# A hybrid decoder block: each head's values projected ahead of its keys, scores kept times -1/8, and the softmax factor taken from two scalars

## The chip, the core and the metric

The kernel is written in a tile language for one NeuronCore of a Trainium2 chip and runs on one of its cores. The metric is the device time of one execution in microseconds (us). The engines named here are TensorE (PE, its weight loads PEld), VectorE (DVE), ScalarE (ACT), GpSimd (POOL) and SyncE (SP, which issues most transfers). Each runs its own queue in order and waits for the others by semaphores.

## The reference, cut to what matters

One layer on 1,024 tokens behind 16 meta tokens (1,040 columns), width 1,024: an RG-LRU branch, a differential attention branch, a gated merge, a squared-ReLU MLP. The change lies in the attention: 8 heads, two key and query parts of 64 columns each (c = 0, 1), 128 value columns, blocks of 128 queries.

```
q = _rope(q, cos, sin);  k = _rope(k, cos, sin)
s = jnp.einsum('bqhcd,bkhcd->bhcqk', q, k) * scale          # scale = 1/8
s = jnp.where(mask, s, finfo.min)
p = jax.nn.softmax(s, axis=-1)
p_diff = p[:, :, 0] - lam * p[:, :, 1]
o = jnp.einsum('bhqk,bkhe->bqhe', p_diff, v)
```

## The kernel before, in words

Every fp32 matmul is made of three, of high and low fp32r parts. A loaded weight tile w_raw is split by POOL: w_hi (L106), then w_lo (L115), two passes over 128x1024. The loads follow a list, `todo`, one tile ahead, so a projection's first matmul sets off the split for the next projection but one tile.

In the attention stage PE's order is the program's own (pinned). For each head, `head_inputs(h)` is a generator of 88 steps, each step three matmuls: 32 for the keys (four chunks of 260 columns), 32 for the values, 24 for the queries (chunks of 504, 260, 260). Keys and queries end in `rope`: ACT copies the last chunk to `raw`, SP swaps halves into `sw` by four transfers, DVE multiplies `raw` by cos (L470), POOL multiplies `sw` by sin (L471) and, for keys, adds the two (L472); then ACT casts the high parts of the keys (L480) and POOL subtracts twice for the low parts (L481, 64x1040 each). The values are copied to `vt` and must be transposed in blocks by PE; an ACT cast and a DVE subtraction (L515, L516) move each group of three out of PSUM. The transposes use the one of two projection banks that the running chunk does not use, and the next chunk needs that bank again.

While head h is attended to, the inputs of head h+1 are woven in as filling: the lists `MAIN`, `MAIN_FIRST`, `MAIN_LAST` and `TAIL` give how many of the steps stand behind each step of the attention. Eighteen (34 at the start) are done before a head's main part begins.

The attention of head h goes by query blocks b = 0 to 7. `scores` makes, for each part c and each piece of up to 512 keys, a matmul pair into one of three score banks; DVE moves the piece out with the mask added and its row maximum kept (L548). A small reduction (L553) and a small multiplication by -1/8 (L554) give the bias, ACT takes the exponentials with row sums (L556), DVE forms a factor from the sums (reciprocal L561, L562) and blends the two parts (L564, both operands in SBUF); the meta columns are cast and subtracted apart (L570, L571, 32 columns). `turn` transposes blended blocks, ACT casts them (L588), DVE subtracts (L589), and `weigh` multiplies them with the values. PE's score of piece n waits until DVE has emptied the score bank of piece n-3.

DVE, ACT, POOL and SP queues are ordered by a scheduler from a model of times; they are in order once built.

Of the kernel before, what the change touches and what calls it, by code (L numbers as in the profile page):

```python
# [13 lines left out]
AF = mybir.ActivationFunctionType  # L14
ALU = mybir.AluOpType
# [3 lines left out]
P = 128  # L19
D = 1024  # L20
# [16 lines left out]
ALL = [(0, 260), (260, 260), (520, 260), (780, 260)]  # L37
REAL = [(NM, 504), (520, 260), (780, 260)]
CH2 = [(0, 512), (512, 512)]
MASK = -3.0e38  # L40
# [30 lines left out]
def hybrid_block(ctx: ExitStack, tc: tile.TileContext, x, meta_tokens, g_mix, w_in, conv_w, conv_b,  # L71
# [3 lines left out]
    V, A, G, PE = nc.vector, nc.scalar, nc.gpsimd, nc.tensor  # L75
# [8 lines left out]
    def f32(ap):  # L84
        return ap.bitcast(F32)
# [15 lines left out]
    def fix(i):  # L101
        if fixed[0]:
# [4 lines left out]
                                                op1=ALU.add)]  # L107
# [11 lines left out]
    todo = []  # L119
# [3 lines left out]
    for d in range(KT):  # L123
        todo += [(w_rnn_out, P * d)] + [(w_in, 5 * D + P * (d + 3))] * (d + 3 < KT)
    for h in range(NH):
        todo += [(w_in, c * D + P * h) for c in (3, 4, 2)]
    todo += [(w_in, 6 * D + P * d) for d in range(KT)]
    todo += [(w_attn_out, P * d) for d in range(KT)]
    todo += [(w_o, j) for j in range(KT // 2)]
# [59 lines left out]
    lam2 = const.tile([P, 2], F32, name="lam2")  # L189
# [20 lines left out]
    sums = [const.tile([P, NH, NB], F32, name=f"sum{c}") for c in range(2)]  # L210
# [4 lines left out]
    with tc.tile_pool(name="hn", bufs=1, reuse_waits="tile") as hnp:  # L215
# [6 lines left out]
        with tc.tile_pool(name="pre", bufs=2) as pre:  # L222
# [19 lines left out]
            for i, (rows, col, src) in enumerate(blocks):  # L242
# [11 lines left out]
                else:  # L254
                    V.scalar_tensor_tensor(out=xg[:rows], in0=xt[:rows], scalar=r[:rows], in1=gbc[:rows],
                                           op0=ALU.mult, op1=ALU.mult)
# [167 lines left out]
        with tc.tile_pool(name="atc", bufs=1, reuse_waits="tile") as atc, \  # L424
# [52 lines left out]
            def set_keys(h, t1):  # L477
                k2 = keys[h] = [at.tile([P, T], F32R, name=f"k2{c}", bufs=2) for c in range(2)]
                for c, (own, oth) in enumerate(halfs):
                    A.copy(out=k2[c][own], in_=t1[own])  # L480
                    G.tensor_tensor(out=k2[c][oth], in0=t1[own], in1=f32(k2[c][own]), op=ALU.subtract)  # L481

            def head_inputs(h):


                yield from rope(h, 3 * D + P * h, ALL, lambda t1: set_keys(h, t1))

                vt = at.tile([P, T], F32, name="raw", bufs=2)
                vm = at.tile([P, 2, 2, NM], F32R, name="vm")

                def use(t0, w, o):
                    A.copy(out=vt[:, t0:t0 + w], in_=o)
                    if t0 == 0:
                        meta = o[:, None, :NM].to_broadcast((P, 2, NM))
                        A.copy(out=vm[:, :, 0, :], in_=meta)
                        V.tensor_tensor(out=vm[:, :, 1, :], in0=meta, in1=f32(vm[:, :, 0, :]), op=ALU.subtract)

                yield from project_by(4 * D + P * h, ALL, take_g, use)
                vv = vals[h] = at.tile([P, NB, 2, P], F32R, name="v", bufs=2)
                for step, _ in enumerate(rope(h, 2 * D + P * h, REAL, lambda t1: rot.update({h: t1}), V)):  # L500
                    yield
                    if step % 8 != 3:
                        continue
                    js = range(step // 8 * 3, step // 8 * 3 + 3)
                    o = take_g(1).rearrange("p (a e) -> p a e", e=P)
                    for i, j in enumerate(js):
                        if j < NB:
                            transpose(o[:, i, :], vt[:, NM + P * j:NM + P * (j + 1)])
                        else:
                            transpose(o[:4 * NM, i, :], f32(vm).rearrange("p a b c -> p (a b c)"))  # L510
                            vt_meta[h] = vmts[h % 2]
                            A.copy(out=vt_meta[h][:4 * NM], in_=o[:4 * NM, i, :])
                    n = min(3, NB - js[0])
                    dst = vv[:, js[0]:js[0] + n]
                    A.copy(out=dst[:, :, 0, :], in_=o[:, :n, :])  # L515
                    V.tensor_tensor(out=dst[:, :, 1, :], in0=o[:, :n, :], in1=f32(dst[:, :, 0, :]), op=ALU.subtract)  # L516

            def queries(h):

# [6 lines left out]
                    V.tensor_tensor(out=qls[c][own], in0=t1[own], in1=f32(q2[c][own]), op=ALU.subtract)  # L526

            def scores(h, b, st):

                L = NM + P * (b + 1)  # L530
                np_ = -(-L // 512)
                cuts = [L * i // np_ // 2 * 2 for i in range(np_ + 1)]
                mx = small.tile([P, 2, 3], F32, name="mx")
                m2 = small.tile([P, 2], F32, name="m2")
                sc = []
                for c in range(2):
                    s = at.tile([P, T], F32, name=f"s{c}", bufs=3 - c)
                    sc.append(s)
                    for i in range(np_):
                        k0, w = cuts[i], cuts[i + 1] - cuts[i]  # L540
                        wa = max(w, 256)
                        o = take_s()
                        matmul(o[:, :wa], lhsT=qls[c][:, P * b:P * (b + 1)], rhs=keys[h][c][:, k0:k0 + wa],
                               start=True, stop=False)
                        matmul(o[:, :wa], lhsT=ques[h][c][:, P * b:P * (b + 1)], rhs=keys[h][c][:, k0:k0 + wa],
                               start=False, stop=True)
                        m0 = MZ + P - w if i == np_ - 1 else 0
                        V.tensor_tensor_reduce(  # L548
                            out=s[:, k0:k0 + w], in0=o[:, :w], in1=mask[:, m0:m0 + w],
                            op0=ALU.add, op1=ALU.max, scale=1.0, scalar=MASK, accum_out=mx[:, c, i:i + 1])  # L550
                        if c == 0 or i < np_ - 1:
                            yield
                V.tensor_reduce(out=m2, in_=mx[:, :, :np_], op=ALU.max, axis=mybir.AxisListType.X)  # L553
                V.tensor_scalar(out=m2, in0=m2, scalar1=-0.125, scalar2=None, op0=ALU.mult)  # L554
                for c in range(2):
                    A.activation(out=sc[c][:, :L], in_=sc[c][:, :L], func=AF.Exp, scale=0.125, bias=m2[:, c:c + 1],  # L556
                                 accum_out=sums[c][:, h, b:b + 1])

                s0, s1 = sc
                cf = small.tile([P, 1], F32, name="cf")  # L560
                V.reciprocal(out=cf, in_=sums[1][:, h, b:b + 1])  # L561
                V.scalar_tensor_tensor(out=cf, in0=sums[0][:, h, b:b + 1], scalar=lam2[:, 0:1], in1=cf,  # L562
                                       op0=ALU.mult, op1=ALU.mult)
                V.scalar_tensor_tensor(out=s0[:, :L], in0=s1[:, :L], scalar=cf, in1=s0[:, :L],  # L564
                                       op0=ALU.mult, op1=ALU.add)
                st[b] = s0

                st["dm", b] = dm = at.tile([P, 2, 2, NM], F32R, name="dm", bufs=3)
                meta = s0[:, None, :NM].to_broadcast((P, 2, NM))
                V.tensor_copy(dm[:, 0], meta)  # L570
                V.tensor_tensor(out=dm[:, 1], in0=meta, in1=f32(dm[:, 0]), op=ALU.subtract)  # L571
                yield
# [492 lines left out]
    with tc.tile_pool(name="mlp", bufs=1, reuse_waits="tile") as ml:  # L1065
# [24 lines left out]
        for c in range(last + 1):  # L1090
            b = {}
# [105 lines left out]
```

## Time and profile before

| what | value |
|---|---|
| three runs, median (lowest, highest) | 1895.49 us (1891.83, 1895.86) |
| the profiled execution: time, span | 1891.57 us, 1889.8 us |
| PE busy over the span | 1786.3 us, 95% |
| DVE, ACT, POOL busy | 1200.3, 800.6, 660.4 us |
| instructions | 25963 |
| mean granted TensorE clock | 0.984 of full speed |

PE is the engine that is nearly always busy, so time is saved or lost where it stands idle or runs at the lower clock. Busy shares of the other engines are averages over stages; whether one of them holds PE up is read from PE's gaps and from what ends them.

### The profile page before, as it was taken

Reading aid. Unit: us, or ns where it says so; the run is one execution under the profiler, and the core shown is the slowest. Engines: PE = TensorE matmul, PEld = TensorE weight load, DVE = VectorE, ACT = ScalarE, POOL = GpSimd, SP = SyncE. Lnnn points to the kernel's source line nnn. Section 1 sums busy time; section 2 is a strip of 40 time slices with the busy share of each in tenths; the row PEclk is TensorE's granted clock in tenths of the full one; section 3 lists DMA queues with packets and bytes.
Section 4 is the critical chain, followed back from the end, with each engine's and each line's share of the span. In section 5 each row is a group of like instructions: output and inputs, shape, how many; then the busy total and the mean of one; then the engine's idle time right before and its main releaser. Section 6 shows DMA issues by size and latency. Waiting matters only on the chain.

```text
span 1889.8 us, 25963 instructions
## 1 busy us (share of the span) xinstructions
PE 1786.3 (95%) x10178; PEld 1565.2 (83%) x10178; DVE 1200.3 (64%) x1829; ACT 800.6 (42%) x1421; POOL 660.4 (35%) x433
## 2 busy tenths in 40 slices
PE   5999999999889989999999999988999988999998
PEld 5999988889789888988889888867888877888876
DVE  7688882112877788788753544475443435888887
ACT  5566660002455545555543210465454453333343
POOL 3243320016332443334312331047656554313220
PEclk9999999999999999999999999999999999999999
DMA  4111112232121122112216535324455568543423
GB/s 158 44 35 46 45 34 73 73 101 82 40 54 43 46 57 60 43 40 54 65 54 253 179 118 191 119 86 161 160 182 172 184 209 301 192 140 133 159 102 119
DMA packets 182236, 208.16 MB, mean 110 GB/s; under 512 B 8048, under 2 KB 137296, under 8 KB 178656
## 3 DMA queue, kind: packets, MB, share of 16 engines
q1 hardware_dynamic: 163376, 171.35, 28.0%
q10 hardware_dynamic: 18736, 35.13, 5.0%
q8 instruction: 80, 1.31, 0.3%
q14 instruction: 44, 0.36, 0.1%
HBM read 147.60 MB, written 50.40 MB: 105 GB/s over the span
## 4 chain that ended last, share of the span: by engine, by line
PE 68%; DVE 19%; issue 6%; ACT 3%; DMA 2%; POOL 1%; SPq 0%; DVEq 0%; POOLq 0%; ACTq 0%
PE bank L155 66%; DVE s L548 2%; PE bank L160 2%; DVE s L564 2%; DVE cf L562 2%; DVE t L470 1%; DVE sl L1100 1%; ACT s L556 1%; DVE ql L526 1%; DMA w_raw<-in_w_in 1%; DVE gate L381 1%; DVE w_lo L115 1%; ACT th L1099 1%; DVE gate L380 0%; DVE m L554 0%
## 5 line engine op out<-in xcount | busy, mean ns | idle before, releaser
L106 POOL TENSOR_SCALAR w_hi<-w_raw 128x1024 fp32r<-128x1024 f32 x77 | 92.0, 1194 | 597.6 <-PE bank L155 471.2
L155 PE MATMUL bank<-act0l,w_hi 128*128 128x260 f32 (+2 forms) x768 | 268.2, 349 | 2.7 <-DVE c L885 2.0
L155 PE MATMUL bank<-act0h,w_lo 128*128 128x260 f32 (+2 forms) x768 | 263.4, 343 | 4.8 <-DVE w_lo L115 4.8
L155 PE MATMUL bank<-act0h,w_hi 128*128 128x260 f32 (+2 forms) x768 | 262.5, 342 | 0.0
L155 PE MATMUL bank<-act1l,w_hi 128*128 128x260 f32 x896 | 255.6, 285 | 0.6 <-POOL w_hi L106 0.6
L155 PE MATMUL bank<-act1h,w_lo 128*128 128x260 f32 x896 | 254.0, 283 | 0.0
L155 PE MATMUL bank<-act1h,w_hi 128*128 128x260 f32 x896 | 253.3, 283 | 0.0
L155 PE MATMUL bank<-th,sl 128*128 128x512 f32 x432 | 169.9, 393 | 1.7 <-DVE sl L1100 1.4
L155 PEld LDWEIGHTS bank<-act1l,w_hi 128*128 128x128 f32 x896 | 169.8, 189 | 2.0 <-POOL w_hi L106 0.9
L155 PEld LDWEIGHTS bank<-act1h,w_lo 128*128 128x128 f32 x896 | 169.6, 189 | 1.2 <-DVE w_lo L115 0.2
L155 PEld LDWEIGHTS bank<-act1h,w_hi 128*128 128x128 f32 x896 | 169.6, 189 | 0.0
L155 PE MATMUL bank<-th,sh 128*128 128x512 f32 x432 | 169.1, 391 | 0.0
L155 PE MATMUL bank<-tl,sh 128*128 128x512 f32 x432 | 162.3, 393 | 4.7 <-DVE tl L1100 4.7
L155 PEld LDWEIGHTS bank<-act0h,w_lo 128*128 128x128 f32 x768 | 147.9, 193 | 19.2 <-DVE w_lo L115 5.6
L155 PEld LDWEIGHTS bank<-act0l,w_hi 128*128 128x128 f32 x768 | 147.8, 192 | 17.9 <-DVE c L885 2.5
L155 PEld LDWEIGHTS bank<-act0h,w_hi 128*128 128x128 f32 x768 | 148.0, 193 | 16.3
L115 DVE TENSOR_TENSOR w_lo<-w_raw,w_hi 128x1024 fp32r<-128x1024 f32 x60 | 83.8, 1396 | 81.3 <-POOL w_hi L106 76.7
L556 ACT ACTIVATE s<-s,m 128x272 f32<-128x272 f32 (+7 forms) x128 | 99.9, 783 | 71.4 <-DVE m L554 71.1
L548 DVE CUSTOM_DVE_ANT_0 s<-bank,mask 128x144 f32<-128x144 f32 (+6 forms) x224 | 109.1, 504 | 31.2 <-PE bank L155 29.7
L155 PE MATMUL bank<-k,ql 128*128 128x256 f32 (+6 forms) x224 | 76.5, 345 | 29.1 <-DVE mx L548 28.4
L1100 DVE TENSOR_TENSOR sl<-s_raw,sh 128x2048 fp32r<-128x2048 f32 x27 | 101.4, 3755 | 0.0
L155 PEld LDWEIGHTS bank<-tl,sh 128*128 128x128 f32 x432 | 81.7, 189 | 22.8 <-DVE tl L1100 5.6
(336 smaller groups left out, 4368.8 us busy)
## 6 DMA issues: line engine op xcount, KB each, us to landing
w_raw<-in_w_in SPq DMA_DIRECT2D x56, 512.0 KB
s_raw<-ff_d SPq DMA_DIRECT2D x27, 1024.0 KB
ff_d<-r ACTq DMA_DIRECT2D x16, 1024.0 KB
b<-in_w_ff SPq DMA_DIRECT2D x16, 1024.0 KB
w_raw<-in_w_ff SPq DMA_DIRECT2D x16, 512.0 KB
s_raw<-in_w_ff SPq DMA_DIRECT2D x16, 512.0 KB
ff_d<-r ACTq DMA_DIRECT2D x31, 256.0 KB
s_raw<-in_w_ff SPq DMA_DIRECT2D x17, 256.0 KB
```

The lines of the kernel that those rows point to most:

```text
L106: hi_part = [lambda out, in_: G.tensor_scalar(out=out, in0=in_, scalar1=1.0, scalar2=0.0, op0=ALU.mult, op1=ALU.add)]
L115: fix(low_part[0].tensor_tensor(out=lo, in0=raw, in1=f32(hi), op=ALU.subtract))
L155: i = PE.matmul(*args, skip_group_check=skip[0], **kw)
L160: i = PE.transpose(o, x, ident[:x.shape[0], :x.shape[0]])
L381: V.tensor_tensor_scan(out=rt, data0=s2, data1=it, initial=0.0, op0=ALU.mult, op1=ALU.add)
L470: V.tensor_tensor(out=t1[:, ts], in0=raw[:, ts], in1=cos[:, ts], op=ALU.mult)
L526: V.tensor_tensor(out=qls[c][own], in0=t1[own], in1=f32(q2[c][own]), op=ALU.subtract)
L548: V.tensor_tensor_reduce(out=s[:, k0:k0 + w], in0=o[:, :w], in1=mask[:, m0:m0 + w], op0=ALU.add, op1=ALU.max, scale=1.0, scalar=MASK, accu ...
L556: A.activation(out=sc[c][:, :L], in_=sc[c][:, :L], func=AF.Exp, scale=0.125, bias=m2[:, c:c + 1], accum_out=sums[c][:, h, b:b + 1])
L562: V.scalar_tensor_tensor(out=cf, in0=sums[0][:, h, b:b + 1], scalar=lam2[:, 0:1], in1=cf, op0=ALU.mult, op1=ALU.mult)
L564: V.scalar_tensor_tensor(out=s0[:, :L], in0=s1[:, :L], scalar=cf, in1=s0[:, :L], op0=ALU.mult, op1=ALU.add)
L1100: ordered(V.tensor_tensor(out=hl[1], in0=src, in1=f32(hl[0]), op=ALU.subtract))
```

## The change

Three edits. In `head_inputs` the values are projected first, and their transposes stand among the keys' 32 steps (behind the fifth, thirteenth and twenty-first) rather than among the queries' 24; the list of loads follows. L548's operation adds the mask, multiplies by -1/8 and keeps the minimum, so the bias needs no multiplication (64 small DVE instructions go), and where one piece covers a block's keys (blocks 0 to 2) no reduction (24 go). L562's product is made by a tensor_scalar with two scalar operands instead of an operation with two tensor operands.

```diff
     for h in range(NH):
-        todo += [(w_in, c * D + P * h) for c in (3, 4, 2)]
+        todo += [(w_in, c * D + P * h) for c in (4, 3, 2)]
...
             def head_inputs(h):
-                yield from rope(h, 3 * D + P * h, ALL, lambda t1: set_keys(h, t1))
-
                 vt = at.tile([P, T], F32, name="raw", bufs=2)
...
                 yield from project_by(4 * D + P * h, ALL, take_g, use)
                 vv = vals[h] = at.tile([P, NB, 2, P], F32R, name="v", bufs=2)
-                for step, _ in enumerate(rope(h, 2 * D + P * h, REAL, lambda t1: rot.update({h: t1}), V)):
+
+                for step, _ in enumerate(rope(h, 3 * D + P * h, ALL, lambda t1: set_keys(h, t1))):
                     yield
-                    if step % 8 != 3:
+                    if step % 8 != 3 or step // 8 == 3:
                         continue
...
                     V.tensor_tensor(out=dst[:, :, 1, :], in0=o[:, :n, :], in1=f32(dst[:, :, 0, :]), op=ALU.subtract)
+                yield from rope(h, 2 * D + P * h, REAL, lambda t1: rot.update({h: t1}), V)
...
-                            op0=ALU.add, op1=ALU.max, scale=1.0, scalar=MASK, accum_out=mx[:, c, i:i + 1])
+                            op0=ALU.add, op1=ALU.min, scale=-0.125, scalar=-MASK, accum_out=mx[:, c, i:i + 1])
...
-                V.tensor_reduce(out=m2, in_=mx[:, :, :np_], op=ALU.max, axis=mybir.AxisListType.X)
-                V.tensor_scalar(out=m2, in0=m2, scalar1=-0.125, scalar2=None, op0=ALU.mult)
+                if np_ > 1:
+                    V.tensor_reduce(out=m2, in_=mx[:, :, :np_], op=ALU.min, axis=mybir.AxisListType.X)
                 for c in range(2):
-                    A.activation(out=sc[c][:, :L], in_=sc[c][:, :L], func=AF.Exp, scale=0.125, bias=m2[:, c:c + 1],
+                    low = m2[:, c:c + 1] if np_ > 1 else mx[:, c, 0:1]
+                    A.activation(out=sc[c][:, :L], in_=sc[c][:, :L], func=AF.Exp, scale=-1.0, bias=low,
                                  accum_out=sums[c][:, h, b:b + 1])
...
-                V.scalar_tensor_tensor(out=cf, in0=sums[0][:, h, b:b + 1], scalar=lam2[:, 0:1], in1=cf,
-                                       op0=ALU.mult, op1=ALU.mult)
+                V.tensor_scalar(out=cf, in0=sums[0][:, h, b:b + 1], scalar1=lam2[:, 0:1], scalar2=cf,
+                                op0=ALU.mult, op1=ALU.mult)
```

What this does to the queues is seen in three places of one head. The first is DVE's queue in the third block of the attention (128x264 are pieces of block 3, s_6708 with 400 columns is block 2). Before:

```order
L470 TENSOR_TENSOR t_6492<-raw,cos 128x1040
L548 ISA s_6786,mx<-bank_6787,mask 128x264
L548 ISA mx 128x1
L548 ISA s_6786,mx<-bank_6791,mask 128x264
L548 ISA mx 128x1
L561 RECIPROCAL cf<-sum_116 128x1
L553 TENSOR_REDUCE m_6747<-mx 128x2
L562 SCALAR_TENSOR_TENSOR cf<-sum_115,lam_81,cf 128x1
L554 TENSOR_SCALAR m_6747<-m_6747 128x2
L564 SCALAR_TENSOR_TENSOR s_6708<-s_6716,cf,s_6708 128x400
```

DVE's queue at the same place with the change (its line numbers differ by one or two: L549 is L548, L566 is L564; s_6672 is block 2, s_6710 block 3, s_6817 the first piece of block 4):

```order
L564 TENSOR_SCALAR cf<-sum_115,lam_81,cf 128x1
L555 TENSOR_REDUCE m_6709<-mx 128x2
L566 SCALAR_TENSOR_TENSOR s_6672<-s_6680,cf,s_6672 128x400
L572 CAST dm<-s_6672 128x32
L573 TENSOR_TENSOR dm<-s_6672,dm 128x32
L563 RECIPROCAL cf<-sum_116 128x1
L564 TENSOR_SCALAR cf<-sum_115,lam_81,cf 128x1
L515 TENSOR_TENSOR v<-bank_6765,v 128x3x128
L566 SCALAR_TENSOR_TENSOR s_6710<-s_6737,cf,s_6710 128x528
L572 CAST dm<-s_6710 128x32
L573 TENSOR_TENSOR dm<-s_6710,dm 128x32
L549 ISA s_6817,mx<-bank_6818,mask 128x328
```

The keys' cosine product has left the place, and the values' first subtraction (L515) now stands there, behind block 3's factor. The second place is DVE's queue where block 5 is blended and block 6 begins (128x784 and 128x456). Before:

```order
L561 RECIPROCAL cf<-sum_116 128x1
L562 SCALAR_TENSOR_TENSOR cf<-sum_115,lam_81,cf 128x1
L548 ISA s_7043,mx<-bank_7044,mask 128x456
L548 ISA mx 128x1
L564 SCALAR_TENSOR_TENSOR s_6956<-s_6968,cf,s_6956 128x784
L548 ISA s_7043,mx<-bank_7065,mask 128x456
```

The same place on DVE with the change:

```order
L564 TENSOR_SCALAR cf<-sum_115,lam_81,cf 128x1
L470 TENSOR_TENSOR t_6724<-raw,cos 128x1040
L566 SCALAR_TENSOR_TENSOR s_6922<-s_6934,cf,s_6922 128x784
L549 ISA s_7021,mx<-bank_7022,mask 128x456
L549 ISA mx 128x1
L549 ISA s_7021,mx<-bank_7042,mask 128x456
L549 ISA mx 128x1
L572 CAST dm<-s_6922 128x32
L549 ISA s_7046,mx<-bank_7047,mask 128x456
L549 ISA mx 128x1
L573 TENSOR_TENSOR dm<-s_6922,dm 128x32
L549 ISA s_7046,mx<-bank_7051,mask 128x456
```

Both the keys' cosine product and block 5's blend now stand ahead of the first move of block 6's scores. The third place is POOL's queue with the change, from the split that the queries' first step sets off (w_hi) on:

```order
L106 TENSOR_SCALAR w_hi<-w_raw 128x1024
L115 TENSOR_TENSOR w_lo<-w_raw,w_hi 128x1024
L471 TENSOR_TENSOR sw<-sw,sin 128x1040
L589 MEMSET pth 128x128
L472 TENSOR_TENSOR t_6724<-t_6724,sw 128x1040
L589 MEMSET ptl 128x128
L481 TENSOR_TENSOR k_6993<-t_6724,k_6993 64x1040
```

Before, the keys' four passes (L471, L472, L481 twice) stood behind the split that the values' first step set off; now they stand behind that of the queries' first step, 32 steps later.

## Rows read from the trace of the kernel before

**Rows 1.** The page's first section: busy us, share of the span, instructions.

```profile
PE 1786.3 (95%) x10178; PEld 1565.2 (83%) x10178; DVE 1200.3 (64%) x1829; ACT 800.6 (42%) x1421; POOL 660.4 (35%) x433
```

**Rows 2.** PE in order of time: start, length, [idle before, releaser].

```profile
483.52 0.90 PE L160 MATMUL bank<-ident,s 128*128 128x128 f32 x3 [3.94 <-DVE s L564]
...
560.24 0.42 PE L155 MATMUL bank<-k,ql 128*128 128x328 f32 x1 [3.69 <-DVE mx L548]
...
683.38 0.40 PE L155 MATMUL bank<-pth,v 128*128 128x256 f32 x2
...
690.94 0.58 PE L155 MATMUL bank<-k,ql 128*128 128x328 f32 x1 [3.65 <-DVE mx L548]
...
702.42 0.28 PE L155 MATMUL bank<-act1h,w_hi 128*128 128x260 f32 x1
...
707.01 0.47 PE L155 MATMUL bank<-k,ql 128*128 128x456 f32 x1 [0.63 <-DVE mx L548]
...
711.47 0.40 PE L155 MATMUL bank<-pth,v 128*128 128x256 f32 x2
...
716.42 0.32 PE L155 MATMUL bank<-k,ql 128*128 128x346 f32 x1
```

**Rows 3.** DVE and POOL in order of time, at the gap before 690.94.

```profile
680.81 2.40 POOL L115 TENSOR_TENSOR w_lo<-w_raw,w_hi 128x1024 fp32r<-128x1024 f32 x1
...
681.00 3.30 DVE L470 TENSOR_TENSOR t<-raw,cos 128x1040 f32<-128x1040 f32 x1
...
684.36 2.43 POOL L471 TENSOR_TENSOR sw<-sw,sin 128x1040 f32<-128x1040 f32 x1 [1.16 <-DVE t L470]
...
685.12 1.69 DVE L562 SCALAR_TENSOR_TENSOR cf<-sum,lam,cf 128x1 f32<-128x1 f32 x1
...
686.85 2.85 DVE L564 SCALAR_TENSOR_TENSOR s<-s,cf,s 128x400 f32<-128x400 f32 x1
686.88 2.39 POOL L472 TENSOR_TENSOR t<-t,sw 128x1040 f32<-128x1040 f32 x1
...
690.38 0.49 DVE L548 CUSTOM_DVE_ANT_0 s<-bank,mask 128x328 f32<-128x328 f32 x1
```

**Rows 4.** Two stretches behind that gap: us, PE, PEld, DVE, ACT, POOL, clock, DMA share, GB/s.

```profile
692.00:694.00 2.00, 2.00 (x12) 2.00 (x11) 2.00 (x10) 0.59 (x1) 0.00 (x0) 0.50 0.00 0
694.00:696.00 2.00, 2.00 (x17) 2.00 (x17) 0.64 (x3) 1.84 (x4) 0.00 (x0) 0.89 0.00 0
```

**Rows 5.** DVE and POOL at the end of the queries' projection, in order of time.

```profile
724.40 1.05 POOL L106 TENSOR_SCALAR w_hi<-w_raw 128x1024 fp32r<-128x1024 f32 x1 [17.73 <-PE bank L155]
724.75 1.77 DVE L470 TENSOR_TENSOR t<-raw,cos 128x1024 f32<-128x1024 f32 x1 [0.52 <-ACT raw L465]
725.54 3.22 POOL L115 TENSOR_TENSOR w_lo<-w_raw,w_hi 128x1024 fp32r<-128x1024 f32 x1
...
727.05 1.99 DVE L622 TENSOR_TENSOR sql<-sq,sqh 128x256 fp32r<-128x256 f32 x1
```

**Rows 6.** Two small DVE operations, all heads: count, shortest/median/longest in ns.

```profile
L562 DVE SCALAR_TENSOR_TENSOR cf<-sum,lam,cf x64: 212/220/2347, 479.6 to 978.3; 128x1 f32<-128x1 f32 x64
...
L570 DVE CAST dm<-s x64: 168/181/2317, 482.4 to 980.1; 128x32 fp32r<-128x32 f32 x64
```

**Rows 7.** Groups by form in one head, 672 to 737: count, busy us, mean ns.

```profile
L562 DVE SCALAR_TENSOR_TENSOR cf<-sum,lam,cf 128x1 f32<-128x1 f32 x8 | 5.9, 737 | 0.2
L589 DVE TENSOR_TENSOR ptl<-bank,pth 128x512 fp32r<-128x512 f32 x6 | 3.9, 680 | 0.0
...
L548 DVE CUSTOM_DVE_ANT_0 s<-bank,mask 128x456 f32<-128x456 f32 x4 | 2.4, 620 | 0.0
...
L554 DVE TENSOR_SCALAR m<-m 128x2 f32<-128x2 f32 x8 | 1.8, 227 | 0.1
...
L564 DVE SCALAR_TENSOR_TENSOR s<-s,cf,s 128x784 f32<-128x784 f32 x1 | 1.0, 1024 | 0.0
...
L556 ACT ACTIVATE s<-s,m 128x912 f32<-128x912 f32 x2 | 2.1, 1050 | 0.5 <-DVE m L554 0.5
```

## The prediction

> **What bounds the kernel now.** I read the busy times first: PE works for 95% of the span, every other engine for less than two thirds [rows 1]. So I looked next, in PE's order of time over the attention stage, for the places where PE stands idle. The reader is to see there a gap of 3.94 us in the first head and then, once a head, one of 3.65 to 3.8 us, of which the first and the fourth head's stand here, always before a score of block 4 that waits for DVE to empty a score bank [rows 2]. A smaller one of 0.63 us stands in block 6. Then I read what DVE and POOL did before the long gap. DVE's cosine product of the keys (L470) is called at 681.00 and takes 3.30 us, while POOL's w_lo runs until 683.21: the product itself is some 1.1 us, the rest is waiting for POOL. The tiny L562 ends with POOL's L471 at 686.8, the blend L564 runs only when L472 is over at 689.27, and the move that PE waits for comes behind it, at 690.38 [rows 3]. A DVE operation with two operands in SBUF and a POOL pass take turns here, whole operation by whole operation. Last the clock: PE runs at half (1.2 of 2.4 GHz) for the two microseconds from 692, and is back during the next two [rows 4]; counted from 690.94 that is about 3.4 us at half, 1.7 us lost. The keys' place therefore costs a head 3.65 + 1.7 = 5.35 us.
>
> **What the change takes away there.** Steps 1 to 14 of a head's main part are now values, so L470, L471, L472 and both L481 leave blocks 3 and 4. POOL keeps w_hi and w_lo there. What is new is the values' first group: its transposes come behind the fifth keys' step, and the ninth step needs that bank back. PE had done eight filling steps when its weigh began at 683.38 [rows 2]; the last of these eight is now that ninth keys' step, so PE asks for the bank at about 683.4. DVE's subtraction for it (L515) is behind block 2's blend, which waits for w_lo until 683.21 [rows 3], behind two small operations, and behind the factor of block 3, whose exponentials I put at an end of about 683.6 (an estimate). That puts its end at about 685.1: a gap of 1.75 us is my value. It is 0 if the blend gets in before w_lo, and as much as the old 3.65 at the other end. I count no loss of clock for it: the rows show half clock only behind 3.65 us. Saved: 5.35 - 1.75 = 3.6 us a head.
>
> **The small operations.** Eight L554 a head (227 ns each) go, and L562 (737 ns in the mean over eight, where its median over all heads is 220) loses an operand [rows 6, 7]. They stand ahead of exponentials and blends on DVE, under PE's work; off the path they are worth nothing. Behind the first place they bring blocks 4 and 5 forward; I give 0.5 us a head, between 0 and the 1.8 us that L554 sums to.
>
> **What the change puts into block 6.** The keys now end just before block 6, where the values ended. Set 0 at the end of that last matmul (702.70 before). PE had used up its three score banks at 706.38, 3.7 us later, and in the old order had to wait only 0.63 us [rows 2]. In the new order of DVE, L470 and block 5's blend stand ahead of the first move of block 6.
>
> L470 meets the w_hi that the same matmul sets off. The queries' end shows this very pairing: L470 waits for w_hi's end, runs, w_lo waits for L470 and then takes 2.2 us of its own, and a later two-operand subtraction waits for w_lo [rows 5]. So w_hi ends at 1.2, L470 at 2.3, w_lo at 4.5, the blend of 784 columns (1.02) at 5.5, the first move (0.62) at 6.1 [rows 7]. PE's fourth score waits 2.4 us.
>
> POOL's L471 follows from 5.5 to 7.9 (2.43) [rows 3], L472 from 8.1 to 10.5. Between the moves stand a 32-column cast and a 32-column subtraction. Such a cast takes 0.18 us alone but up to 2.3 us behind POOL [rows 6]; here the cast is held to 7.9 and the subtraction to 10.5. So the fourth move ends at 11.3 and the subtraction L589 for the transposed blocks (0.68 [rows 7], behind another that I put at 0.4) at 12.5. PE needs 4.46 us from its fourth score to that weigh, of which 0.3 were transposes now done earlier [rows 2]: it is there at 10.2 and waits 2.3 us.
>
> The exponentials of block 6 (two of 1.05) run from 11.5 to 13.7, behind them a cast on ACT and the next L589, to 14.9; PE is there at 13.5 and waits 1.4 us. Then the blend to 16.0, and POOL's two key passes (2.43 each, rows 7) to 18.4 and 21.0; the next cast waits for the first, the next subtraction for the second, with block 7's first moves behind each. The second ends at 21.7. From that weigh to block 7's fifth score PE has 4.95 us of its own [rows 2], 18.9 with the gap so far: 2.8 us more.
>
> Together 2.4 + 2.3 + 1.4 + 2.8 = 8.9 us of gaps where there were 0.63: 8.3 more. Against 3.6 and 0.5 a head is 4.2 us longer. No half clock is counted behind these gaps; if gaps of 2.4 us bring it too, up to 1.7 us a head more shows, since most of it would lie under the next wait. If the small subtractions slip through between two passes, about 3 us a head less. SP's transfers move with the keys: four swaps behind the same copy, landing before POOL is free of w_lo, so they cost nothing; were they 1 us later, L471 would start that much later. The keys themselves are due only a head's tail later: cover of some 15 us.
>
> **The sum.** Six heads weave the next head's inputs by the same list: 6 x 4.2 = 25 us. The first head has its own list, with the keys at blocks 0 to 2 before and at block 5 now: it loses 3.94 us and a half clock of about 1.7, and takes on up to 8.3; I put 0, between -5.6 and +8.3. The last head weaves no keys: 0, at best -1.8. The profiled execution took 1891.6 us, span 1889.8: 1891.6 + 25 = 1917 us. It stands 3.9 us under the median of the runs, at their lower end; I leave the sum as it is.
>
> **Rivals.** *The waits go with the operand (faster).* Place: the factor before each blend. If what holds L562 up is its second operand, and the blends find POOL between passes, eight factors give DVE back 8 x (0.737 - 0.220) = 4.1 us a head [rows 6, 7], the moves behind them come in time at block 6 too, and both of PE's gaps go: 6 x (5.35 + 0.63) = 36 us, 1856 us; with a part of it, 1870 to 1885. It decides whether block 6's first move ends by 3.7 us after the keys' last matmul. Against it: the blend at 686.85 waited 2.4 us right behind an L562 that had waited too [rows 3], and L470 now stands in front. The Trainium skill (SBUF — State Buffer, "Who interferes with whom") says that a DVE instruction with two SBUF inputs contends with a GpSimd instruction that reads SBUF, and one with at most one SBUF input outside the two-port modes does not; the trace agrees for L470 and the blend, and no row here shows the new form of the factor. By that rule the factor stops waiting, which is what this rival builds on. Chance 0.2.
>
> *The blend gets in before w_lo (slower, but little).* If DVE keeps its turn behind L470, block 5's blend ends at 3.4, the first move at 4.0 and the fourth score hardly waits; the rest of the walk comes 2.6 us earlier. A head is 1.6 us longer, 1902 us. Against it: at 726.5 POOL had the next turn [rows 5]. Chance 0.14.
>
> *The two places cancel (no change).* Block 6 costs what block 4 gave, if the small operations slip through and the values' bank is free at once: 1888 to 1895 us. Chance 0.12, and 0.02 more of a small gain.
>
> **How the numbers follow.** My forecast has 0.52, and its own range is 1903 to 1936: at the lower end the bounds of the small operations, at the upper the clock (6 x 1.7) and the first head's 8.3. A difference of 0.2% (3.8 us) is about what runs of this kernel can tell from none. Slower: 0.52 + 0.14 = 0.66; same: 0.12; faster: 0.2 + 0.02 = 0.22. For 8 in 10 the range takes in the cancelling case and the milder half of the fast one: 1874 to 1936, leaving out about 0.12 below and 0.06 above.
>
> **What will show it.** Right: no gap before block 4's score but one of 1 to 2.5 us at a projection matmul waiting for DVE's L515; gaps in block 6's fourth score, the weigh behind it and block 7, together 6 to 10 us a head; casts or subtractions of 32 columns with 1 to 2 us there; factors at 0.2 us. Wrong: L470 in block 6 at 1.1 us with w_lo behind the blend, or PE without gaps from block 6 on, or DVE's waits there with PE still covered by its filling steps.

## The result, and the profile after

The changed kernel takes 1920.7 us (median of four runs, 1919.21 to 1924.38), the kernel before 1893.94 us: a ratio of 1.0151 with a 95% interval of [1.0139, 1.0162], 1.5% slower. The profiled execution took 1924.38 us. First the page's busy times, which answer to [rows 1]:

```profile
PE 1796.7 (93%) x10178; PEld 1569.8 (82%) x10178; DVE 1204.4 (63%) x1741; ACT 805.6 (42%) x1421; POOL 666.3 (35%) x433
```

DVE has 88 operations fewer and is no less busy: a waiting operation counts as busy. PE's gaps over half a microsecond up to block 7's scores, in the head that starts at 689, follow with the keys' last matmul (start, length, [idle before, releaser]), as in [rows 2]:

```profile
702.85 0.39 PE L155 MATMUL bank<-act0l,w_hi 128*128 128x260 f32 x1 [1.46 <-DVE v L515]
...
717.50 0.28 PE L155 MATMUL bank<-act1h,w_hi 128*128 128x260 f32 x1
...
723.68 0.47 PE L155 MATMUL bank<-k,ql 128*128 128x456 f32 x1 [2.23 <-DVE mx L549]
...
729.67 0.39 PE L155 MATMUL bank<-ptl,v 128*128 128x256 f32 x1 [1.44 <-DVE ptl L591]
731.43 0.50 PE L155 MATMUL bank<-pth,v 128*128 128x256 f32 x2 [0.69 <-ACT pth L590]
738.47 0.42 PE L155 MATMUL bank<-k,ql 128*128 128x346 f32 x1 [1.90 <-DVE mx L549]
```

The 3.65 us before block 4's score are gone. In their place stand 1.46 us at the values' bank and, in this head, 6.3 us in blocks 6 and 7, where 0.63 stood. DVE and POOL at the beginning of block 6, in order of time:

```profile
718.23 1.78 DVE L470 TENSOR_TENSOR t<-raw,cos 128x1040 f32<-128x1040 f32 x1
719.93 3.14 DVE L566 SCALAR_TENSOR_TENSOR s<-s,cf,s 128x784 f32<-128x784 f32 x1
723.00 0.62 DVE L549 CUSTOM_DVE_ANT_0 s<-bank,mask 128x456 f32<-128x456 f32 x1
...
724.11 1.43 DVE L572 CAST dm<-s 128x32 fp32r<-128x32 f32 x1
725.31 0.62 DVE L549 CUSTOM_DVE_ANT_0 s<-bank,mask 128x456 f32<-128x456 f32 x1
...
725.86 2.08 DVE L573 TENSOR_TENSOR dm<-s,dm 128x32 fp32r<-128x32 f32 x1
727.86 0.62 DVE L549 CUSTOM_DVE_ANT_0 s<-bank,mask 128x456 f32<-128x456 f32 x1
...
717.88 1.05 POOL L106 TENSOR_SCALAR w_hi<-w_raw 128x1024 fp32r<-128x1024 f32 x1 [16.52 <-PE bank L155]
719.01 3.24 POOL L115 TENSOR_TENSOR w_lo<-w_raw,w_hi 128x1024 fp32r<-128x1024 f32 x1
...
722.55 2.81 POOL L471 TENSOR_TENSOR sw<-sw,sin 128x1040 f32<-128x1040 f32 x1 [0.30 <-DMA sw<-raw]
...
725.46 2.43 POOL L472 TENSOR_TENSOR t<-t,sw 128x1040 f32<-128x1040 f32 x1
```

The turns are seen in the ends: L470 ends behind w_hi (720.0), w_lo gets the next turn and ends at 722.25, the blend of 1.02 us [rows 7] ends right behind it at 723.07. The cast then ends with L471, the subtraction with L472, each with a move queued behind it. Counted from the end of the keys' last matmul (717.8), the blend ends at 5.3, the cast at 7.8 and the subtraction at 10.2, where the prediction's walk had 5.5, 7.9 and 10.5. Three small operations over all heads (count, shortest/median/longest in ns), as in [rows 6]:

```profile
L564 DVE TENSOR_SCALAR cf<-sum,lam,cf x64: 268/272/276, 483.6 to 1010.5; 128x1 f32<-128x1 f32 x64
...
L572 DVE CAST dm<-s x64: 161/181/2552, 484.8 to 1012.1; 128x32 fp32r<-128x32 f32 x64
...
L573 DVE TENSOR_TENSOR dm<-s,dm x64: 180/192/2125, 485.7 to 1012.4; 128x32 fp32r<-128x32 f32 x64
```

The new factor never waits. Before, 21 of the 64 factors took over 0.9 us, 33.9 us in sum, and one cast and one subtraction over 1.2 us; now 16 casts and 15 subtractions take over 1.2 us, 59.8 us in sum. These are lengths, the operations' own work included.

The table gives the attention stage of each profiled execution, read from PE's order of time: when the first head's first score starts, how long the first head lasts, the mean of the six heads behind it, the rest from the last head's first score to the span's end, and per head of the six PE's idle time and what the half clock took (1 less the granted clock, summed over windows of 1 us).

| kernel | first score at | first head | a head of six | rest | idle a head | half clock a head |
|---|---|---|---|---|---|---|
| before | 472.5 | 68.7 | 65.33 | 956.6 | 5.05 | 1.71 |
| changed | 478.4 | 71.7 | 69.89 | 953.2 | 8.24 | 1.71 |
| e1_small | 473.9 | 62.7 | 68.33 | 952.5 | 7.03 | 2.84 |
| e2_order | 477.1 | 70.3 | 73.86 | 954.8 | 10.57 | 4.83 |
| e3_trans_in_queries | 476.2 | 65.6 | 69.00 | 951.8 | 7.16 | 1.99 |
| e4_factor | 474.8 | 69.8 | 64.90 | 953.4 | 4.36 | 1.99 |
| e5_min | 474.0 | 65.2 | 68.28 | 953.7 | 7.54 | 1.99 |
| e6_keys_on_dve | 475.2 | 66.0 | 67.92 | 951.5 | 6.31 | 2.56 |
| e7_meta_off_dve | 478.6 | 67.5 | 64.67 | 954.0 | 4.12 | 1.71 |
| e8_w_lo_dve | 478.4 | 66.9 | 67.07 | 950.1 | 6.80 | 1.14 |
| e9_old_keys_dve | 474.7 | 64.7 | 63.61 | 957.4 | 3.81 | 0.85 |
| e10_old_both_dve | 473.6 | 71.5 | 66.93 | 953.1 | 5.76 | 2.56 |
| e11_new_both_dve | 474.7 | 62.1 | 64.99 | 950.3 | 4.72 | 1.14 |
| e12_new_all | 473.6 | 64.6 | 65.05 | 950.9 | 4.50 | 1.42 |

Between before and after the span grew by 32.8 us: 5.9 ahead of the first score, 3.0 in the first head, 27.3 in the six (4.6 each), less 3.4 behind. The medians differ by 26.8; before's profiled execution lies 2.4 under its median, that of after 3.7 above its own.

### The profile page after: what moved, and what is told of

Its sections match the earlier page's. It is cut to its first block, busy times and chain, and to the rows that moved or that the text cites. A ratio compares the mean times of both kernels' runs of the same rounds, so it can differ in the third digit from the quotient of the medians.

```text
span 1922.6 us, 25897 instructions
## 1 busy us (share of the span) xinstructions
PE 1796.7 (93%) x10178; PEld 1569.8 (82%) x10178; DVE 1204.4 (63%) x1741; ACT 805.6 (42%) x1421; POOL 666.3 (35%) x433
## 4 chain that ended last, share of the span: by engine, by line
PE 64%; DVE 20%; issue 6%; ACT 5%; DMA 3%; POOL 2%; SPq 0%; DVEq 0%; POOLq 0%; ACTq 0%
PE bank L155 62%; DVE s L549 2%; DVE s L566 2%; ACT s L558 2%; DVE dm L573 2%; DVE dm L572 2%; PE bank L160 1%; DVE sl L1102 1%; DMA w_raw<-in_w_in 1%; DVE t L470 1%; DVE ql L526 1%; DVE gate L381 1%; DVE ptl L591 1%; DVE w_lo L115 1%; DMA r<-in_w_ff 1%
## 5 line engine op out<-in xcount | busy, mean ns | idle before, releaser
L155 PE MATMUL bank<-act0l,w_hi 128*128 128x260 f32 (+2 forms) x768 | 268.2, 349 | 10.2 <-DVE v L515 8.7
L549 DVE CUSTOM_DVE_ANT_0 s<-bank,mask 128x144 f32<-128x144 f32 (+6 forms) x224 | 109.3, 504 | 34.0 <-PE bank L155 32.2
L558 ACT ACTIVATE s<-s,m 128x528 f32<-128x528 f32 (+4 forms) x80 | 75.4, 945 | 63.1 <-DVE m L555 63.1
```

Of the source, the lines that this page charges most:

```text
L155: i = PE.matmul(*args, skip_group_check=skip[0], **kw)
L549: V.tensor_tensor_reduce(out=s[:, k0:k0 + w], in0=o[:, :w], in1=mask[:, m0:m0 + w], op0=ALU.add, op1=ALU.min, scale=-0.125, scalar=-MASK, ...
```

## Experiments

My theory was that of the prediction: DVE and POOL take turns, and the keys' new place puts the turns with w_lo and the keys' passes before block 6's moves. The rivals were that the small edits or the values' transposes make the loss, that the factor's waits go with its operand, and that DVE is simply full. Ratios are to the kernel before, with their 95% intervals.

**The two small edits alone (e1_small), the order alone (e2_order).** The diff of the change, split in two: e1_small has the min/-1/8 edit and the two-scalar factor in the old order of projections, e2_order the new order with the old small operations.

```diff
-        todo += [(w_in, c * D + P * h) for c in (3, 4, 2)]
+        todo += [(w_in, c * D + P * h) for c in (4, 3, 2)]
```

Expected of e1_small:

> The order of before with the two small edits alone (scores kept times -1/8, the factor from two scalars). Theory: they are worth 0.5 us a head in six heads, so some 3 us less than before, between 0 and 8. Rival A (the waits go with the operand): the factor's waits of 4 us a head go and nothing takes them over, PE's gap before block 4 shrinks to under 2 us, 25 us less than before. Rival B (the new small operations themselves cost): 10 us or more longer than before.

Measured: 1900.86 us, 1.0037 [1.0024, 1.0049]: slower, where a gain was expected. Block 4's gap stays at 3.7 us, so rival A fails. Expected of e2_order:

> The new order of a head's inputs alone, with the small operations of before. Theory: the whole slowdown and the 3 us that the small operations save, so 30 us longer than before, between 25 and 38, with PE's gaps at block 6, its weigh and block 7. Rival B (the small operations cost): within 8 us of before.

Measured: 1947.56 us, 1.0283 [1.0267, 1.0299], 53 us where some 30 were expected. So the loss is the order's, but the two halves are not a sum: the small edits cost 6.6 us in the old order and save 27 in the new one. By the table they save 4.0 us a head there, with 2.3 less of idle time and 3.1 less of half clock (together more than 4.0; how the two overlap is not shown). Which of the two small edits does it is not shown, since neither was run alone in the new order. The new order's part is seen in DVE and POOL of e2_order in the head at 694 (L555 is the old multiplication by -1/8, which the change removes):

```profile
732.77 1.89 DVE L572 TENSOR_TENSOR dm<-s,dm 128x32 fp32r<-128x32 f32 x1
734.59 0.68 DVE L590 TENSOR_TENSOR ptl<-bank,pth 128x512 fp32r<-128x512 f32 x1
735.19 2.12 DVE L555 TENSOR_SCALAR m<-m 128x2 f32<-128x2 f32 x1
...
734.87 2.42 POOL L472 TENSOR_TENSOR t<-t,sw 128x1040 f32<-128x1040 f32 x1
```

A product of two columns is held for a whole POOL pass (seven of the 64 take over 1.2 us), and block 6's exponentials stand behind it. L590, with one operand in PSUM, takes its usual 0.68 us beside POOL's passes.

**Which of the small edits costs in the old order (e4_factor, e5_min).** Each alone in the kernel before.

```diff
-                V.scalar_tensor_tensor(out=cf, in0=sums[0][:, h, b:b + 1], scalar=lam2[:, 0:1], in1=cf,
+                V.tensor_scalar(out=cf, in0=sums[0][:, h, b:b + 1], scalar1=lam2[:, 0:1], scalar2=cf,
```

Expected of e4_factor:

> The kernel before with the factor alone made from two scalars; DVE's queue keeps nearly its old order. Theory (the wait belongs to POOL's turn, and the next operation with two SBUF operands takes it): the factor never waits, the blend behind it does, block 6's first move, which stands between the two, comes 1.3 us earlier and its gap of 0.64 us goes, block 4's 3.7 us stay: 1888 to 1893 us. Rival (waits go with the operand): the blends do not take them over, block 4's gap falls under 2 us: below 1880 us. Rival (this edit is what made the small edits cost 6.6 us together): 1898 us or more.

Measured: 1890.44 us, 0.9977 [0.9967, 0.9986]: as the theory had it. Before, the factor ends with w_lo after 1.53 us:

```profile
704.88 1.53 DVE L562 SCALAR_TENSOR_TENSOR cf<-sum,lam,cf 128x1 f32<-128x1 f32 x1
...
703.98 2.41 POOL L115 TENSOR_TENSOR w_lo<-w_raw,w_hi 128x1024 fp32r<-128x1024 f32 x1
```

In e4_factor it takes 0.27, the first move of block 6 follows at once, and the blend behind it takes the wait over (1.02 us of work), with POOL's w_lo beside it:

```profile
706.28 0.27 DVE L562 TENSOR_SCALAR cf<-sum,lam,cf 128x1 f32<-128x1 f32 x1
706.57 0.63 DVE L548 CUSTOM_DVE_ANT_0 s<-bank,mask 128x456 f32<-128x456 f32 x1
...
707.12 2.47 DVE L564 SCALAR_TENSOR_TENSOR s<-s,cf,s 128x784 f32<-128x784 f32 x1
...
706.35 2.41 POOL L115 TENSOR_TENSOR w_lo<-w_raw,w_hi 128x1024 fp32r<-128x1024 f32 x1
```

Block 6's gap of 0.64 us is gone in all six heads, block 4's is not (3.4 to 3.9). The gain comes from where the turn falls, not from the wait being saved: with the factor alone changed, nine casts (before, one) and seven products by -1/8 (before, one) take over 1.2 us. Expected of e5_min:

> The kernel before with the minimum and the factor -1/8 inside the move alone; 88 small DVE operations fewer, and the scheduler orders DVE anew (block 5's blend ahead of block 6's first move, a values' subtraction behind block 7's factor). Theory: that new order is what the small edits cost: gaps of about 1.5 us before block 6's score and 1 us at the values' subtraction, 1897 to 1904 us. Rival (the factor's form costs): within 3 us of the kernel before. Rival (88 operations less is time gained): 1885 us or less.

Measured: 1904.45 us, 1.0051 [1.0038, 1.0064], a little above the range's 1904. It is this one of the two that costs: with 88 operations fewer the scheduler sets block 5's blend ahead of block 6's first move, and a values' subtraction behind block 7's factor. Block 6's gap is 1.7 us and a new one of 1.0 us stands at the subtraction:

```profile
708.72 1.40 DVE L563 SCALAR_TENSOR_TENSOR cf<-sum,lam,cf 128x1 f32<-128x1 f32 x1
710.16 1.03 DVE L565 SCALAR_TENSOR_TENSOR s<-s,cf,s 128x784 f32<-128x784 f32 x1
711.11 0.62 DVE L548 CUSTOM_DVE_ANT_0 s<-bank,mask 128x456 f32<-128x456 f32 x1
```

In e1_small, with the blend in the same place, the factor takes 0.27 us, the blend 2.32, and the gap is 1.46: with the blend ahead of the move, the move waits for POOL whichever of the two is held.

**The values' transposes back among the queries' steps (e3_trans_in_queries).**

```diff
-                for step, _ in enumerate(rope(h, 3 * D + P * h, ALL, lambda t1: set_keys(h, t1))):
+                yield from rope(h, 3 * D + P * h, ALL, lambda t1: set_keys(h, t1))
+                for step, _ in enumerate(rope(h, 2 * D + P * h, REAL, lambda t1: rot.update({h: t1}), V)):
```

> The changed kernel, but the values' transposes stand among the queries' steps again; values are still projected ahead of keys. Theory: only PE's wait of 1.45 us a head for the bank behind the first group goes, six times, so 8 us less than the changed kernel, and 18 longer than before; the gaps in blocks 6 and 7 stay. Rival C (the transposes among the keys' steps are what costs): within 6 us of before.

Measured: 1908.2 us, 1.0076 [1.0062, 1.0089], 12.5 us under the changed kernel. The bank's gap of 1.46 us is gone, but a head of the six gains only 0.9: the last group's subtraction has gaps of 0.4 to 1.0 us in three of the heads, and the half clock takes 0.28 us a head more. Over half of the gain lies ahead of the first score and in the first head (8.3 us): a step near the expected size, mostly for another reason.

**The keys' POOL passes on DVE (e6_keys_on_dve), w_lo on DVE (e8_w_lo_dve), the small pair of cast and subtraction off DVE (e7_meta_off_dve),** each alone in the changed kernel. First the keys:

```diff
-                        G.tensor_tensor(out=sw[:, ts], in0=sw[:, ts], in1=sin[:, ts], op=ALU.mult)
-                        E.tensor_tensor(out=t1[:, ts], in0=t1[:, ts], in1=sw[:, ts], op=ALU.add)
+                        (V if E is G else G).tensor_tensor(out=sw[:, ts], in0=sw[:, ts], in1=sin[:, ts], op=ALU.mult)
+                        V.tensor_tensor(out=t1[:, ts], in0=t1[:, ts], in1=sw[:, ts], op=ALU.add)
...
-                    G.tensor_tensor(out=k2[c][oth], in0=t1[own], in1=f32(k2[c][own]), op=ALU.subtract)
+                    V.tensor_tensor(out=k2[c][oth], in0=t1[own], in1=f32(k2[c][own]), op=ALU.subtract)
```

> The changed kernel, but the keys' sine product, their sum and their two low parts run on DVE, none on POOL: 4.5 us more work a head for DVE, 9.7 less for POOL. Theory (waits for POOL's passes): block 6 and 7 lose the waits of the cast, the subtraction and the blend behind those passes, about 8 us of DVE a head, so the time falls by 3 us a head, about 18 us under the changed kernel (10 to 28). Rival D (DVE has simply more to do in those blocks than it can): 4.5 us a head longer, 25 us over the changed kernel.

Measured: 1899.32 us, 1.0031 [1.0019, 1.0043], 21 us under the changed kernel, within the range, but only in part as the theory had it: a head of the six gains 2.0 us where 3 were expected (the half clock takes 0.85 more), and 8.8 us lie ahead of the first score and in the first head. The gaps of 1.44, 0.69 and 1.90 us give way to two of 0.9 and 1.0; the bank's and the fourth score's stay at 1.46 and 2.23, since w_lo is still on POOL and holds the blend as before:

```profile
708.78 3.14 DVE L566 SCALAR_TENSOR_TENSOR s<-s,cf,s 128x784 f32<-128x784 f32 x1
...
714.25 1.24 DVE L471 TENSOR_TENSOR sw<-sw,sin 128x1040 f32<-128x1040 f32 x1
...
707.86 3.24 POOL L115 TENSOR_TENSOR w_lo<-w_raw,w_hi 128x1024 fp32r<-128x1024 f32 x1
```

The weights' low parts in the attention:

```diff
-            low_part[0] = G
+            low_part[0] = V
```

> The changed kernel with the weights' low parts on DVE instead of POOL in the attention (24 passes of some 1.2 us). Theory (w_lo holding block 2's and block 5's blend makes the gaps at the values' bank, 1.46 us, and at block 6's fourth score, 2.23 us): the first goes, the second falls to some 1.4 since the scheduler puts w_lo ahead of the move, the gaps behind block 6's moves stay: 1900 to 1911 us. Rival (DVE has no room, the gaps are its own work): 3.6 us a head more on it, 1921 us or more.

Measured: 1897.13 us, 1.0016 [1.0007, 1.0025], 3 us under the range: the two gaps did what was expected (none, and 1.23 to 1.25 us). What went beyond it lies in the first head (4.8 us shorter), behind the six (3.1) and in fewer half clocks. Two gaps grew: the weigh's in block 6 to 1.9 us, and one late in five of the heads from 0.7 to between 1.9 and 2.3.

The small pair:

```diff
-                V.tensor_copy(dm[:, 0], meta)
-                V.tensor_tensor(out=dm[:, 1], in0=meta, in1=f32(dm[:, 0]), op=ALU.subtract)
+                A.copy(out=dm[:, 0], in_=meta)
+                G.tensor_tensor(out=dm[:, 1], in0=meta, in1=f32(dm[:, 0]), op=ALU.subtract)
```

> The changed kernel with the 32-column cast on ACT and the 32-column subtraction on POOL instead of DVE. Theory (a cast or a subtraction of 32 columns is held for a whole POOL pass, 1.4 and 2.1 us in block 6 and again in block 7, and the moves behind it make the gaps of 1.44 us at the weigh and 1.89 us at block 7's score): both fall under 0.7 us, the values' bank (1.46) and the fourth score (2.23) keep theirs, 2 to 3 us a head: 1900 to 1910 us. Rival (the next two-operand operation takes the wait over, or POOL's subtraction comes too late for the transposes): 1916 us or more.

Measured: 1887.05 us, 0.9964 [0.9951, 0.9978]. The theory named the right place and was short in size: 34 us under the changed kernel, where at most 21 were expected. POOL keeps all its passes. Block 6 of its head at 675:

```profile
703.36 1.78 DVE L470 TENSOR_TENSOR t<-raw,cos 128x1040 f32<-128x1040 f32 x1
705.07 3.15 DVE L566 SCALAR_TENSOR_TENSOR s<-s,cf,s 128x784 f32<-128x784 f32 x1
708.14 0.62 DVE L549 CUSTOM_DVE_ANT_0 s<-bank,mask 128x456 f32<-128x456 f32 x1
...
709.24 0.62 DVE L549 CUSTOM_DVE_ANT_0 s<-bank,mask 128x456 f32<-128x456 f32 x1
...
709.80 0.63 DVE L549 CUSTOM_DVE_ANT_0 s<-bank,mask 128x456 f32<-128x456 f32 x1
...
708.54 0.26 POOL L573 TENSOR_TENSOR dm<-s,dm 128x32 fp32r<-128x32 f32 x1 [1.16 <-ACT dm L572]
708.75 2.41 POOL L471 TENSOR_TENSOR sw<-sw,sin 128x1040 f32<-128x1040 f32 x1
...
710.55 0.90 DVE L624 TENSOR_TENSOR sql<-sq,sqh 128x256 fp32r<-128x256 f32 x1
```

The fourth score keeps its gap (2.23), but the four moves now end at 710.43 while L471 runs beside them: a move from PSUM waits for no POOL pass. Every gap behind it in blocks 6 and 7 is gone, and the values' bank's falls to 1.0. DVE's next operation with two SBUF operands (L624) ends just behind L471 and takes 0.90 us, where it took 0.41 before: half a microsecond of wait went on to it, with no move behind it that PE waits for. A head is 5.2 us shorter, 4.1 of it idle time of PE; the other 1.1 the trace does not show as idle. Matmuls' ends are modelled in the profile, so short waits can lie beneath them; that they do is not shown.

**The same remedies in the old order, and both together (e9_old_keys_dve, e10_old_both_dve, e11_new_both_dve, e12_new_all).** The edits are those of e6_keys_on_dve and e8_w_lo_dve; e12_new_all has that of e7_meta_off_dve too.

> The kernel before with the keys' four POOL passes (sine product, sum, two low parts) on DVE. Theory (turns with POOL's passes make the old gap before block 4's score): no L562 or blend over 1.5 us there, the gap falls from 3.65 us to between 0.5 and 2, about 2 to 3 us a head: 1874 to 1884 us. Rival (the four passes, 1.24 us each on DVE, stand ahead of the same move and take as long): 1892 to 1903 us.

Measured: 1879.95 us, 0.9914 [0.9901, 0.9928], in the range. Block 4's gap fell to 2.17 us, and in three of the six heads no half clock followed.

> The kernel before with the keys' four POOL passes and the weights' low parts on DVE in the attention. Theory (what is left of block 4's gap, 2.17 us with the keys' passes on DVE, is the cosine product's 2 us behind w_lo, against 1.2 us of w_lo's own on DVE): about 1 us a head under the keys' passes alone, 1868 to 1877 us. Rival (DVE is full by now): 1882 us or more.

Measured: 1902.45 us, 1.0046 [1.0034, 1.0058]: the theory missed and the time is the rival's. The trace shows an order rather than a full DVE: block 4's gap did fall, to 0.6 to 0.8 us, but the scheduler put w_lo, L471 and L472 ahead of the blends, and PE then waits 3.0 us a head for block 3's:

```profile
694.17 0.42 PE L155 MATMUL bank<-k,ql 128*128 128x328 f32 x1 [0.58 <-DVE mx L548]
697.87 0.90 PE L160 MATMUL bank<-ident,s 128*128 128x128 f32 x3 [3.02 <-DVE s L564]
```

> The changed kernel with the keys' four POOL passes and the weights' low parts on DVE in the attention. Theory (both of the new order's waits are POOL's turns): the gap at the values' bank goes, the fourth score's falls to 1.2 us, the others stay under 1 us: 1878 to 1888 us. Rival (block 6 is too short for the keys' work whoever does it): no better than with one of the two moved, 1896 us or more.

Measured: 1879.16 us, 0.9923 [0.991, 0.9936], as the theory had it: with no large two-operand pass against another, block 6 has room for the keys. The gap at the values' bank is gone; in blocks 6 and 7 are left:

```profile
698.18 0.47 PE L155 MATMUL bank<-k,ql 128*128 128x456 f32 x1 [1.24 <-DVE mx L549]
...
703.27 0.39 PE L155 MATMUL bank<-ptl,v 128*128 128x256 f32 x1 [0.55 <-DVE ptl L591]
...
709.98 0.43 PE L155 MATMUL bank<-k,ql 128*128 128x348 f32 x1 [1.01 <-DVE mx L549]
```

The rival that DVE is simply full fails: with the keys' passes and the low parts added to it, DVE is busy for 1189.1 us, in the changed kernel for 1204.4.

> The changed kernel with all three taken together: keys' passes and the weights' low parts on DVE, the 32-column cast on ACT and the 32-column subtraction on POOL. If what is left of block 6's gaps is DVE's own work, the 3 us a head of small operations it loses show at two of the four gaps left (0.55 and 1.01 us), 1 us a head and something in the first head: 1870 to 1877 us, below all others. If those small operations cost only by their waits, which are gone already, nothing is added to the run with both on DVE: 1877 to 1882 us. If POOL's and DVE's one remaining meeting counts, over 1882 us.

Measured: 1882.42 us, 0.9942 [0.9929, 0.9956], on the border of its second and third case. Once POOL's passes are gone, moving the small pair adds nothing: a head of the six takes 65.05 us against 64.99. So in e7_meta_off_dve it was the pair's waits that counted, not its work on DVE. Whether the meeting that is left costs the 3 us more than in e11_new_both_dve stays open; the two intervals overlap.

e9_old_keys_dve and e11_new_both_dve beat both kernels, the one before by 0.9% and 0.8%; their intervals overlap, so neither order is shown to be the better once the keys are on DVE.

## Why the prediction was right, and where it was not

**The direction and the place were right.** The forecast was 1917 us, measured are 1920.7. The old gap went and block 6 took on more, by turns of DVE and POOL: e6_keys_on_dve, e8_w_lo_dve and e7_meta_off_dve each take one side of a turn away, and the gaps named for that turn go or shrink. The walk's first step, "PE's fourth score waits 2.4 us", measured 2.23, and the values' bank, "a gap of 1.75 us", measured 1.46. Behind them the walk was too long: 1.44 or nothing for 2.3 at the weigh, 0.69 for 1.4 at the next, 1.90 for 2.8 in block 7; 4.8 to 6.3 us in place of 8.9, where "6 to 10" was to be the sign. The old gap's reading was a little narrow: over the six heads it is 3.63 to 3.88 us. The key passes' 2.43 us stand in [rows 3], not in rows 7, and are those of L471 and L472; and the second rival's sum comes to 1901, not 1902. None of this moves the forecast.

**"Saved: 5.35 - 1.75 = 3.6 us a head" was too much: the clock.** I counted the 1.7 us at half clock as gone with the gap; behind the new ones, "No half clock is counted", though 1.7 us a head more was named should it come. The granted clock behind the gap of 1.90 us (us, PE, PEld, DVE, ACT, POOL, clock, DMA share, GB/s), as in [rows 4]:

```profile
737.00:739.00 2.00, 0.53 (x3) 0.53 (x4) 2.00 (x6) 0.00 (x0) 0.93 (x1) 1.00 0.00 0
739.00:741.00 2.00, 2.00 (x14) 2.00 (x13) 1.42 (x7) 0.48 (x1) 0.00 (x0) 0.71 0.00 0
741.00:743.00 2.00, 2.00 (x11) 2.00 (x10) 0.04 (x1) 1.93 (x4) 0.00 (x0) 0.50 0.00 0
```

It moved from block 4 to block 6 (three heads, behind the gap of 2.23 us) or 7 (three heads, behind that of 1.90) and takes 1.71 us a head as before. So a head's 4.6 us are 3.2 of idle time, 1.4 that the trace shows neither as idle time nor as clock, and nothing of the clock, where I had 8.3 - 3.6 - 0.5 = 4.2. That 4.2 came near 4.6 is luck: the new gaps add 4.2 to 5.6 us, not 8.3; the old place gives back 3.65 - 1.46 = 2.2, not 3.6; and the 1.4 had no term.

**"I give 0.5 us a head" for the small operations was mis-sized, and its reason failed.** "Off the path they are worth nothing" treats them by their duration. They can be worth the POOL pass that they are caught in (L555 above) and the order that the scheduler makes without them: 27 us gained in the new order, 6.6 us lost in the old.

**"First head ... I put 0, between -5.6 and +8.3" failed.** The head itself took 3.0 us more, inside these bounds (the upper one leaves out the 5.6 us that it was to lose; with them it is 2.7), but 5.9 us more lie ahead of its first score, where the sum had no term. I looked at its own list of filling, not at its inputs, which run ahead of the attention. There POOL's keys' passes now stand directly before the queries'. The queries' L471 before, then POOL and PE in the changed kernel:

```profile
465.23 2.40 POOL L471 TENSOR_TENSOR sw<-sw,sin 128x1024 f32<-128x1024 f32 x1
```

```profile
466.34 2.42 POOL L481 TENSOR_TENSOR k<-t,k 64x1040 fp32r<-64x1040 f32 x1
...
468.84 2.39 POOL L115 TENSOR_TENSOR w_lo<-w_raw,w_hi 128x1024 fp32r<-128x1024 f32 x1
471.19 2.40 POOL L471 TENSOR_TENSOR sw<-sw,sin 128x1024 f32<-128x1024 f32 x1
...
478.39 0.58 PE L155 MATMUL bank<-k,ql 128*128 128x256 f32 x1 [4.10 <-DVE ql L526]
```

Six microseconds lie between the two starts of L471. In the gap of 4.10 us the clock fell to half (columns as above), and over the first head half clock takes 7.8 us where it took 5.1 before: 2.7 more, close to the head's 3.0:

```profile
478.00:486.00 8.00, 5.75 (x24) 5.45 (x25) 6.42 (x16) 2.29 (x8) 2.85 (x3) 0.50 0.22 66
```

With the keys' passes on DVE the first score starts at 475.2 and no such gap is left. The last head, put at 0, gained 3.4 us with its tail, about what e1_small gains there (4.1). So of the 32.8 us by which the profiled span grew, 27.3 lie in the six heads that the sum priced at 25, and what it put at 0 adds 5.5.

**The rivals.** "The waits go with the operand" had the half of it right: the factor does not wait. The Trainium skill (SBUF — State Buffer, "Who interferes with whom") says that a DVE instruction with at most one SBUF input, outside the 2-port modes, does not contend with GpSimd; 268 to 276 ns in 64 of 64 agree. But in the old order the waits go on to blends, casts and products by -1/8 (e4_factor). In the new order there was little to hand on: in e2_order, which has the old factor, no factor takes over 0.94 us, and four casts and fourteen subtractions already take over 1.2, 36.9 us in sum. So the 59.8 us come from the order first, not from the factor's waits. "The blend gets in before w_lo" is refuted by 719.93 3.14 above, "the two places cancel" by the interval.

## What to carry to other kernels

Where two engines take turns on whole operations, price a small operation by the other engine's pass that it can be caught in, and ask what is queued behind it; keep such operations away from the moves that PE waits for. Taking a wait off one operation can give it to the next one that needs the turn, as in e4_factor: it is a gain only if less hangs on that one, as in e7_meta_off_dve. When a scheduler sets the order, an edit that removes work is also an edit of the order, and each half of a change is to be run alone before their effects are added.

## What the hardware showed unexpectedly

A cast of 128x32 with one operand in SBUF is held as long as an operation with two (1.43 and 1.95 us in a head, up to 2.55), and so is a product of 128x2 (2.12), while the product of 128x1 with two scalars never is. With POOL's passes moved (e11_new_both_dve) no cast takes over 0.28 us. The Trainium skill (SBUF — State Buffer, "Who interferes with whom") lists copies, casts and tensor_scalar among those that can enter the 2-port modes and then contend with GpSimd, so the first two agree with it; what spares the 128x1 form no run here tells apart. The same product of 128x1040 takes 2.43 us on POOL and 1.24 on DVE. The half clock is not settled: with 5.05 us of idle time a head it came once a head before, with 7.03 in e1_small ten times in six heads, with 6.80 in e8_w_lo_dve four times.
